# Attention heads in pairs between a layer's products, on one core

## Chip, core and metric

One core of one Trainium2 chip runs one layer of a decoder. The metric is the device time of one execution in microseconds; the median of the runs counts. TensorE is the engine of matrix products, VectorE, ScalarE and GpSimd work on tiles, SyncE issues the transfers of weights. In the profile they are PE (PEld: its weight loads), DVE, ACT, POOL and SP.

## What is computed

256 positions of width 2048, batch 1, float32. The reference, cut to what matters:

```python
h = rmsnorm(x, mix_norm_g)
qkv = h @ w_in                              # 2048 x 6144: q, k, v of group A, then of group B
q_a, k_a = partial_rope(q_a), partial_rope(k_a)     # first quarter of each head, 8 heads of 128
o_a = moba_attention(q_a, k_a, v_a)         # 256 positions are one block: causal softmax
o_b = stick_breaking_attention(q_b, k_b, v_b)       # 8 heads, no softmax, strictly causal
x = x + concat(rmsnorm(o_a, moba_out_g), rmsnorm(o_b, sb_out_g)) @ w_out
x = x + square(relu(rmsnorm(x, mlp_norm_g) @ w_up)) @ w_down
out = rmsnorm(x, final_norm_g)
```

## The kernel before

**Products.** All weights come in items of 512 rows by 512 columns, one step for each. Item i+3 is fetched into `raw` while item i is worked on. Each weight is split into a high and a low float32r part: ScalarE writes `wh` (`split_hi`, L122), VectorE writes the rest `wl` (`split_lo`, L128), each in two halves of an item, two items ahead of the products (LOOK = 2). In `w_stationary` (q, k and w_up; L234, L235) the weights are loaded into TensorE and the activations stream, 16 pairs of products a step; in `x_stationary` (v, w_out, w_down; L250 to L252) it is the other way round, 24 products a step. The products add up in six buffers `acc` of PSUM.

**Order.** The order of the work is written out by hand (`manual_schedule`); each engine runs its own instructions in the order in which they were issued, and waits only for data and buffers. `step` issues an item: half of its products, what hangs on hook 2i, the split of the first half of item i+2 on VectorE, the other half of the products, what hangs on hook 2i+1, the split of the second half. `at(slot, f, ...)` hangs f on a hook, and it is issued there on all engines that it uses. So what a hook issues on VectorE stands in VectorE's queue ahead of the split that follows.

**Heads.** The heads go in four groups of four: stick-breaking heads 0 to 3 and 4 to 7 (gi = 0, 1), then MoBA heads 0 to 3 and 4 to 7 (gi = 2, 3). Each group has 12 items, four of q, four of v, four of k. Its attention runs during the 12 items of the next group, hung on hooks counted from i0, the hook in the middle of the first of them: hooks 0 to 7 belong to q's items, 8 to 15 to v's, 16 to 23 to k's. The fourth group's attention runs among the items of w_out (eight for each half of the heads; hooks 0 to 15 are the first eight). A head's attention is in three places on TensorE:

- `probs` (L339 to L369): `scores` (L333, L334), four matmuls that take q and k; then for stick-breaking two sigmoids on ScalarE, causal masks on GpSimd, scans and a product on VectorE (L351, L354; the scanned tiles `stay` and `cum` have one buffer), and for MoBA the softmax: mask and scale (L361), maxima (L363), exponentials on ScalarE (L364), reciprocal (L366), scaling (L368);
- `turn` (L375): three transposes of the probabilities, copied out by ScalarE (L377);
- `values` (L385, L386): four matmuls with v, then the output's split and its squares for the norm on ScalarE, VectorE and GpSimd (L391 to L395).

Each place takes a buffer of `att`, of which there are two.

**q and k.** When a q or k item group ends, `qk_out` (L318, L319) puts the sums of each head into qT or kT. `qk_scale` multiplies them by the norm's factor on GpSimd (L329); for MoBA heads it first rotates the first 32 dimensions on VectorE (L325 to L328, four instructions on 32 partitions). For k's head 0 it is issued at once, for heads 1 to 3 it hangs on a hook ahead of the head's scores.

Before the change these hooks were, with `gap, d1, d2 = (3, 4, 5) if gi == 3 else (4, 5, 7)`:

```python
at(2 * state["i"] + gap * m - 1, qk_scale, dst, m, rope)     # k, heads 1 to 3
at(i0 + 2 + gap * m, probs, qT, kT, m, box)
at(i0 + 2 + gap * m + d1, turn, m, box, tbox)
at(i0 + 2 + gap * m + d2, values, g, h, m, vs, tbox)
```

In the first three groups that gives scores at hooks 2, 6, 10, 14, turnings at 7, 11, 15, 19, values at 9, 13, 17, 21 and k's scaling at 3, 7, 11; in the fourth, scores at 2, 5, 8, 11, turnings at 6, 9, 12, 15, values at 7, 10, 13, 16 and k's scaling at 2, 5, 8. A residual add of w_out (`o_out`, L448) is issued by the products themselves, ahead of the hook that follows them.

Of the kernel before, what the change touches and what calls it, by code (L numbers as in the profile page):

```python
# [49 lines left out]
def layer(ctx: ExitStack, tc, x, mix_g, w_in, moba_g, sb_g, w_out, mlp_g, w_up, w_down, fin_g,  # L50
# [84 lines left out]
    def rms_scale(r, ss, n):  # L135

        nc.vector.tensor_scalar(r, ss, 1.0 / n, EPS, op0=ALU.mult, op1=ALU.add)
        nc.gpsimd.tensor_tensor(r, r, mhalf[:, :r.shape[-1]], op=ALU.pow)
# [86 lines left out]
    def w_stationary(i, ps, j, nj, done):  # L225

        wh, wl = parts[i]
        mk = [(m, k) for m in range(4) for k in range(KI)]
        if i < 3:
            mk = [(m, k) for k in range(KI) for m in range(4)]  # L230
        for n, (m, k) in enumerate(mk):
            kt = j * KI + k
            first, last = j == 0 and k == 0, j == nj - 1 and k == KI - 1
            nc.tensor.matmul(ps[m], wh[:, k, m * P:(m + 1) * P], actT[:, kt, :], start=first, stop=False)  # L234
            nc.tensor.matmul(ps[m][:, S:2 * S], wl[:, k, m * P:(m + 1) * P], actT[:, kt, 0:S],  # L235
                             start=False, stop=last)
            if last:
                done(m)
            if n == (3 if i < 3 else 7) or (i == 0 and n == 7):
                yield  # L240
        parts.pop(i)
# [14 lines left out]
    def x_stationary(i, ps, j, nj, xT, k0, done):  # L256
        for t in range(2):
            x_part(i, ps, j, nj[t], xT, k0, t, done)
            if t == 0:
                yield  # L260
        parts.pop(i)
# [4 lines left out]
    def at(slot, f, *a):  # L266

        hooks.setdefault(slot, []).append((f, a))
# [5 lines left out]
    state = {"i": 0}  # L274

    def step(work):
        i = state["i"]
        state["i"] += 1
        fetch(i + 3)
        h0, h1 = slice(0, KI // 2), slice(KI // 2, KI)  # L280
        ahead = i + LOOK if i >= LOOK else len(items)
        if i > LOOK:
            split_hi(ahead, h0)
        for part, _ in enumerate(work(i)):
            run_hooks((i, part) if part else 2 * i)
            split_hi(ahead, h1 if i > LOOK else slice(0, KI))
            split_lo(ahead, h0)
        run_hooks(2 * i + 1)
        split_lo(ahead, h1)
        del raws[i]  # L290
# [13 lines left out]
    with ExitStack() as phase:  # L304
# [10 lines left out]
        def qk_out(dst, ps, m):  # L315

            low = aw.tile([P, S], F32, name="low")
            nc.scalar.copy(low, ps[:, S:2 * S])  # L318
            nc.vector.tensor_add(dst[:, m, :], ps[:, 0:S], low)  # L319

        def qk_scale(dst, m, rope):

            if rope:
                rot = aw.tile([32, 2, S], F32, name="rot", bufs=1)
                nc.vector.stream_shuffle(rot[:, 0], dst[:32, m, :], [(r + HALF) % 32 for r in range(32)])  # L325
                nc.vector.tensor_mul(rot[:, 0], rot[:, 0], sinr)
                nc.vector.tensor_mul(rot[:, 1], dst[:32, m, :], cosr)
                nc.vector.tensor_add(dst[:32, m, :], rot[:, 0], rot[:, 1])  # L328
            nc.gpsimd.tensor_mul(dst[:, m, :], dst[:, m, :], r1b)  # L329
# [67 lines left out]
        def group_scale(g):  # L397
# [3 lines left out]
            nc.vector.tensor_copy(rg[:, g, :], ps[:, 0:2])  # L401
            rms_scale(rg[:, g, :], rg[:, g, :], DG)

        for gi, (g, h) in enumerate(((1, 0), (1, 1), (0, 0), (0, 1))):
            rope = g == 0
            gap, d1, d2 = (3, 4, 5) if gi == 3 else (4, 5, 7)
            qT = qkvp.tile([P, 4, S], F32, name="qT")
            kT = qkvp.tile([P, 4, S], F32, name="kT")
            vs = qkvp.tile([P, 2, CW], F32, name="vs")
            def v_out(t):  # L410
                if t == 0:
                    nc.scalar.activation(vs[:, 0, :], ps[0], AF.Copy, scale=r1[:, 0:1])
                else:
                    nc.vector.tensor_scalar(vs[:, 1, :], ps[1], r1[:, 1:2], None, op0=ALU.mult)

            def head_out(kind, m):
                dst = qT if kind == "q" else kT
                qk_out(dst, ps[m], m)
                if kind == "q":
                    at(2 * state["i"] + (6 if gi == 0 else 0) + 2 * m, qk_scale, dst, m, rope)  # L420
                elif m == 0:
                    qk_scale(dst, m, rope)
                else:
                    at(2 * state["i"] + gap * m - 1, qk_scale, dst, m, rope)

            for kind in "qvk":
                ps = [acc.tile([P, 512], F32, name="acc") for _ in range(2 if kind == "v" else 4)]
                for j in range(4):
                    if kind == "v":
                        step(lambda i: x_stationary(i, ps, j, (4, 4), actT, 0, v_out))  # L430
                    else:
                        step(lambda i: w_stationary(i, ps, j, 4, lambda m: head_out(kind, m)))
            box, tbox = {}, {}
            i0 = 2 * state["i"]
            probs = probs_moba if g == 0 else probs_sb
            for m in range(4):
                at(i0 + 2 + gap * m, probs, qT, kT, m, box)
                at(i0 + 2 + gap * m + d1, turn, m, box, tbox)
                at(i0 + 2 + gap * m + d2, values, g, h, m, vs, tbox)
            if h == 1:  # L440
                at(i0 + 2 + gap * 3 + d2 + 2, group_scale, g)


        ssx = op.tile([P, 2, 4], F32, name="ssx")
# [133 lines left out]
```

## Time and profile before

| what | before |
|---|---|
| median of 3 runs | 1108.91 us (1108.74 to 1108.95) |
| the profiled execution | 1109.04 us, its span 1107.3 us |
| TensorE busy | 1096.8 us, 99% of the span |
| VectorE, ScalarE, GpSimd busy | 634.0, 506.4, 130.3 us (57%, 46%, 12%) |
| chain that ended last | TensorE 97%, transfers 1% |
| granted clock of TensorE, mean | 0.998 |
| transfers | 207.96 MB, 188 GB/s in the mean |

Matmuls follow each other before the one ahead has ended, so what a product costs is read from the start of one to the start of the next, not from its duration. In brackets at a row's end stands how long the engine was idle before it and what ended that. A row of a timeline that stands for several equal instructions ends in their number (x3), and its duration is that of all of them.

### The profile page before, as it was taken

To read this page: it belongs to the slowest core of one execution; us is meant where nothing else is said; L and a number is where in the kernel's file an instruction comes from. 1 tells how busy PE (TensorE), PEld (TensorE's weight loads), DVE (VectorE), ACT (ScalarE), POOL (GpSimd) and SP (SyncE) were. 2 spreads that over 40 slices of the span, in tenths; PEclk is the share of its full clock that TensorE was granted. 3 is DMA by queue.
4 is the path that set the end of the run, shared out by engine and by line. 5 is a ranking of instruction groups with operands and counts; after the bars stand their busy time and mean duration, and the time that the engine had idled before them with its cause. 6 is when DMAs were issued, how large, how long until landed. Compare 5 with 4: busy or idle time off the path is not lost.

```text
span 1107.3 us, 14123 instructions
## 1 busy us (share of the span) xinstructions
PE 1096.8 (99%) x5672; PEld 938.3 (85%) x5672; DVE 634.0 (57%) x818; ACT 506.4 (46%) x735; POOL 130.3 (12%) x154
## 2 busy tenths in 40 slices
PE   8999999999999999999999999999999999999997
PEld 7888888888888888888888888888888888888886
DVE  5655657668676665655564444445655565455453
ACT  5645444455444554544453333334444544344342
POOL 0101213224111002211220000001111211000000
PEclk9999999999999999999999999999999999999999
DMA  8755454554545554666457546554665456555642
GB/s 304 243 163 181 155 188 156 188 190 153 184 158 190 187 192 154 213 225 206 154 174 245 190 155 226 190 190 152 207 214 188 152 207 212 190 200 188 207 165 76
DMA packets 104673, 207.96 MB, mean 188 GB/s; under 512 B 3440, under 2 KB 4512, under 8 KB 104480
## 3 DMA queue, kind: packets, MB, share of 16 engines
q1 hardware_dynamic: 103376, 204.49, 54.5%
q10 hardware_dynamic: 1232, 2.58, 0.7%
q8 instruction: 44, 0.72, 0.3%
q14 instruction: 21, 0.17, 0.0%
HBM read 204.96 MB, written 2.10 MB: 187 GB/s over the span
## 4 chain that ended last, share of the span: by engine, by line
PE 97%; DMA 1%; issue 0%; ACT 0%; SPq 0%; DVE 0%; POOLq 0%; POOL 0%; ACTq 0%
PE acc L234 31%; PE acc L235 16%; PE acc L252 16%; PE acc L250 16%; PE acc L251 16%; DMA raw<-in_w_in 1%; PE att L334 1%; PE att L385 1%; PE att L375 0%; PE att L150 0%; PE att L386 0%; PE att L333 0%; SPq L113 0%; ACT xs L522 0%; DVE wl L128 0%
## 5 line engine op out<-in xcount | busy, mean ns | idle before, releaser
L128 DVE TENSOR_TENSOR wl<-raw,wh 128x1024 fp32r<-128x1024 f32 (+1 forms) x386 | 461.5, 1231 | 198.0 <-ACT wh L122 198.0
L122 ACT ACTIVATE wh<-raw 128x1024 fp32r<-128x1024 f32 (+1 forms) x385 | 389.5, 1051 | 351.0 <-PE acc L252 202.0
L234 PE MATMUL acc<-actT,wh 128*128 128x512 f32 x1536 | 536.8, 394 | 0.6 <-ACT wh L122 0.6
L235 PE MATMUL acc<-actT,wl 128*128 128x256 f32 x1536 | 429.9, 280 | 0.4 <-DVE wl L128 0.4
L234 PEld LDWEIGHTS acc<-actT,wh 128*128 128x128 f32 x1536 | 288.4, 188 | 63.9 <-ACT wh L122 0.9
L235 PEld LDWEIGHTS acc<-actT,wl 128*128 128x128 f32 x1536 | 288.6, 188 | 1.3 <-DVE wl L128 1.0
L250 PE MATMUL acc<-wh,uT 128*128 128x512 f32 (+1 forms) x520 | 200.7, 386 | 0.0
L251 PE MATMUL acc<-wl,uT 128*128 128x512 f32 (+1 forms) x520 | 200.7, 386 | 0.0
L252 PE MATMUL acc<-wh,uT 128*128 128x512 f32 (+1 forms) x520 | 200.7, 386 | 0.0
L488 POOL TENSOR_TENSOR uT<-u,uT 128x256 fp32r<-128x256 f32 x64 | 61.3, 958 | 510.0 <-ACT uT L487 510.0
L251 PEld LDWEIGHTS acc<-wl,uT 128*128 128x128 f32 x520 | 97.7, 188 | 19.8
L250 PEld LDWEIGHTS acc<-wh,uT 128*128 128x128 f32 x520 | 97.7, 188 | 19.7
L252 PEld LDWEIGHTS acc<-wh,uT 128*128 128x128 f32 x520 | 97.7, 188 | 19.4
L485 DVE TENSOR_TENSOR u<-acc,ulow 128x256 f32<-128x256 f32 x64 | 27.2, 425 | 99.7 <-ACT ulow L484 89.8
L487 ACT ACTIVATE uT<-u 128x256 fp32r<-128x256 f32 x64 | 26.8, 418 | 67.0 <-DVE u L486 67.0
L250 PE MATMUL acc<-wh,actT 128*128 128x512 f32 x128 | 52.6, 411 | 0.0
L250 PE MATMUL acc<-wh,oT 128*128 128x512 f32 x128 | 51.8, 405 | 0.0
L252 PE MATMUL acc<-wh,actT 128*128 128x512 f32 x128 | 50.2, 392 | 0.0
L252 PE MATMUL acc<-wh,oT 128*128 128x512 f32 x128 | 50.1, 391 | 0.0
L251 PE MATMUL acc<-wl,actT 128*128 128x512 f32 x128 | 49.9, 390 | 0.0
L251 PE MATMUL acc<-wl,oT 128*128 128x512 f32 x128 | 49.9, 390 | 0.0
L491 DVE SCALAR_TENSOR_TENSOR xs<-acc,r,xs 128x512 f32<-128x512 f32 (+1 forms) x18 | 13.0, 720 | 43.2 <-PE acc L252 43.2
(106 smaller groups left out, 574.4 us busy)
## 6 DMA issues: line engine op xcount, KB each, us to landing
raw<-in_w_up SPq DMA_DIRECT2D x64, 1024.0 KB, 6.1
raw<-in_w_down SPq DMA_DIRECT2D x64, 1024.0 KB, 5.1
raw<-in_w_in SPq DMA_DIRECT2D x47, 1024.0 KB, 5.2
raw<-in_w_out SPq DMA_DIRECT2D x16, 1024.0 KB, 5.0
xs<-in_x SPq DMA_DIRECT2D x3, 512.0 KB, 9.1
raw<-in_w_in SPq DMA_DIRECT2D x4, 256.0 KB, 5.7
fgb<-in_final_norm_g ACTq DMA_DIRECT2D x1, 1024.0 KB
out<-xs SPq DMA_DIRECT2D x4, 256.0 KB, 2.4
```

Source lines behind the costliest of these rows:

```text
L122: nc.scalar.activation(parts[i][0][:, ks], raws[i][:, ks], AF.Copy)
L128: nc.vector.tensor_sub(wl[:, ks], raws[i][:, ks], wh[:, ks].bitcast(F32))
L234: nc.tensor.matmul(ps[m], wh[:, k, m * P:(m + 1) * P], actT[:, kt, :], start=first, stop=False)
L235: nc.tensor.matmul(ps[m][:, S:2 * S], wl[:, k, m * P:(m + 1) * P], actT[:, kt, 0:S], start=False, stop=last)
L250: nc.tensor.matmul(ps[t][:, :cols.stop - cols.start], hi, wh[:, k, cols], start=first, stop=False)
L251: nc.tensor.matmul(ps[t][:, :cols.stop - cols.start], hi, wl[:, k, cols], start=False, stop=False)
L252: nc.tensor.matmul(ps[t][:, :cols.stop - cols.start], lo, wh[:, k, cols], start=False, stop=last)
L334: nc.tensor.matmul(ps[:, P:3 * P], qT[:, m, P:S], kT[:, m, :], start=True, stop=True)
L485: nc.vector.tensor_add(u, ps[:, 0:S], low)
L487: nc.scalar.activation(hi, u, AF.Copy)
L488: nc.gpsimd.tensor_sub(lo, u, hi.bitcast(F32))
L491: nc.vector.scalar_tensor_tensor(xs[:, t, c0:c1], ps[:, :c1 - c0], r2[:, t:t + 1], xs[:, t, c0:c1], op0=ALU.mult, op1=ALU.add)
```

## The change

The hooks of the four groups come from a table, by pairs of heads. Heads 0 and 1 have their scores at one hook, their turnings at one hook and their values at one hook, and so have heads 2 and 3: in the first three groups at hooks 2, 7, 16 and 5, 17, 19, in the fourth at 2, 8, 10 and 5, 11, 14. That makes 6 places of a group in place of 12. The scaling of k's heads 1, 2 and 3 hangs on hooks 1, 3 and 4. The norm of a group's output (`group_scale`) follows two hooks after the last values, as before.

```diff
+        WHEN = (((2, 7, 16), (5, 17, 19)), ((2, 8, 10), (5, 11, 14)))
         for gi, (g, h) in enumerate(((1, 0), (1, 1), (0, 0), (0, 1))):
             rope = g == 0
-            gap, d1, d2 = (3, 4, 5) if gi == 3 else (4, 5, 7)
+            when = WHEN[gi == 3]
...
                 elif m == 0:
                     qk_scale(dst, m, rope)
                 else:
-                    at(2 * state["i"] + gap * m - 1, qk_scale, dst, m, rope)
+                    at(2 * state["i"] + (0, 1, 3, 4)[m], qk_scale, dst, m, rope)
...
             probs = probs_moba if g == 0 else probs_sb
-            for m in range(4):
-                at(i0 + 2 + gap * m, probs, qT, kT, m, box)
-                at(i0 + 2 + gap * m + d1, turn, m, box, tbox)
-                at(i0 + 2 + gap * m + d2, values, g, h, m, vs, tbox)
+            for pair, (t_probs, t_turn, t_values) in enumerate(when):
+                for m in (2 * pair, 2 * pair + 1):
+                    at(i0 + t_probs, probs, qT, kT, m, box)
+                    at(i0 + t_turn, turn, m, box, tbox)
+                    at(i0 + t_values, values, g, h, m, vs, tbox)
             if h == 1:
-                at(i0 + 2 + gap * 3 + d2 + 2, group_scale, g)
+                at(i0 + t_values + 2, group_scale, g)
```

How the instructions then stand, engine by engine. VectorE in the third group (gi = 2, MoBA) before, from the end of head 0's softmax to the start of head 1's; L128 is a split, L325 to L328 the rotation of a k head, L319 puts q's sums into qT:

```order
L368 TENSOR_SCALAR prob<-prob,st 128x256
L128 TENSOR_TENSOR wl<-raw,wh 128x1024
L325 STREAM_SHUFFLE rot<-kT 32x256
L326 TENSOR_TENSOR rot<-rot,cst 32x256
L327 TENSOR_TENSOR rot<-kT,cst 32x256
L328 TENSOR_TENSOR kT<-rot 32x256
L128 TENSOR_TENSOR wl<-raw,wh 128x1024 x3
L319 TENSOR_TENSOR qT<-acc,low 128x256 x2
L361 SCALAR_TENSOR_TENSOR prob<-att,cst 128x384
```

One rotation, head 1's, lay between two softmaxes, with four splits and two sums around it. VectorE at the same place with the change, from the start of head 1's softmax to the start of head 2's:

```order
L361 SCALAR_TENSOR_TENSOR prob<-att,cst 128x384
L363 TENSOR_REDUCE st<-prob 128x1 x2
L366 RECIPROCAL st<-st 128x2
L368 TENSOR_SCALAR prob<-prob,st 128x128
L368 TENSOR_SCALAR prob<-prob,st 128x256
L128 TENSOR_TENSOR wl<-raw,wh 128x1024
L325 STREAM_SHUFFLE rot<-kT 32x256
L326 TENSOR_TENSOR rot<-rot,cst 32x256
L327 TENSOR_TENSOR rot<-kT,cst 32x256
L328 TENSOR_TENSOR kT<-rot 32x256
L128 TENSOR_TENSOR wl<-raw,wh 128x1024
```

Head 0's softmax, the same five rows, stands directly ahead of these. The rotation shown is head 2's; behind the last row come head 3's four rows, one more split, and then the softmax of head 2. Head 1's rotation has moved ahead of head 0's softmax.

VectorE in the fourth group (among w_out's items) with the change, from the split behind head 2's rotation on; L452 is the residual add, L448 before:

```order
L128 TENSOR_TENSOR wl<-raw,wh 128x1024
L452 SCALAR_TENSOR_TENSOR xs<-acc,rg,xs 128x512
L325 STREAM_SHUFFLE rot<-kT 32x256
L326 TENSOR_TENSOR rot<-rot,cst 32x256
L327 TENSOR_TENSOR rot<-kT,cst 32x256
L328 TENSOR_TENSOR kT<-rot 32x256
L128 TENSOR_TENSOR wl<-raw,wh 128x1024
L452 SCALAR_TENSOR_TENSOR xs<-acc,rg,xs 128x512
L361 SCALAR_TENSOR_TENSOR prob<-att,cst 128x384
```

The first row is the split behind head 2's rotation, the rotation shown is head 3's, and the last row begins head 2's softmax. Before, the piece of the queue with head 3's rotation was this (L393 is of a head's values):

```order
L393 SCALAR_TENSOR_TENSOR oT<-att,g_85,oT 128x256
L128 TENSOR_TENSOR wl<-raw,wh 128x1024
L325 STREAM_SHUFFLE rot<-kT 32x256
L326 TENSOR_TENSOR rot<-rot,cst 32x256
L327 TENSOR_TENSOR rot<-kT,cst 32x256
L328 TENSOR_TENSOR kT<-rot 32x256
L361 SCALAR_TENSOR_TENSOR prob<-att,cst 128x384
```

Head 3's rotation stood ahead of head 2's softmax, three hooks ahead of head 3's own scores, and no residual add lay between the split and the rotation; now it stands one hook ahead of its scores, behind the softmaxes of heads 0 and 1 and a residual add.

On TensorE, the first scores of the third group then stand as two heads' in a row between L235 and L234, and the scores of heads 2 and 3 three half steps behind them; each head's scores wait for GpSimd's multiplication of its own k alone.

## Rows read from the trace of the kernel before

**Rows 1.** The page: busy time by engine, and the chain that ended last.

```profile
PE 1096.8 (99%) x5672; PEld 938.3 (85%) x5672; DVE 634.0 (57%) x818; ACT 506.4 (46%) x735; POOL 130.3 (12%) x154
...
PE 97%; DMA 1%; issue 0%; ACT 0%; SPq 0%; DVE 0%; POOLq 0%; POOL 0%; ACTq 0%
```

**Rows 2.** Waits of TensorE: who for whom, us in total, times, longest us.

```profile
PE acc L203 <- POOL mhalf L81: 1.5, 1, 1.5
...
PE att L150 <- DVE actT L156: 0.4, 1, 0.4
```

**Rows 3.** TensorE's timeline, scores, then turning: start us, us, instruction.

```profile
98.43 0.38 PE L333 MATMUL att<-kT,qT 128*128 128x128 f32 x2
...
99.32 0.28 PE L235 MATMUL acc<-actT,wl 128*128 128x256 f32 x1
...
139.18 0.28 PE L235 MATMUL acc<-actT,wl 128*128 128x256 f32 x1
...
139.87 0.28 PE L235 MATMUL acc<-actT,wl 128*128 128x256 f32 x1
```

**Rows 4.** The same at scores, third and then fourth group, heads 0 and 1.

```profile
233.22 0.38 PE L333 MATMUL att<-kT,qT 128*128 128x128 f32 x2
...
244.97 0.38 PE L333 MATMUL att<-kT,qT 128*128 128x128 f32 x2
...
306.14 0.38 PE L333 MATMUL att<-kT,qT 128*128 128x128 f32 x2
...
314.99 0.38 PE L333 MATMUL att<-kT,qT 128*128 128x128 f32 x2
```

**Rows 5.** The page, groups: busy us, mean ns of one, idle before.

```profile
L250 PE MATMUL acc<-wh,uT 128*128 128x512 f32 (+1 forms) x520 | 200.7, 386 | 0.0
...
L250 PE MATMUL acc<-wh,actT 128*128 128x512 f32 x128 | 52.6, 411 | 0.0
```

**Rows 6.** VectorE's timeline, third group, then fourth: softmax, splits, rotation, residual add.

```profile
234.07 0.56 DVE L361 SCALAR_TENSOR_TENSOR prob<-att,cst 128x384 f32<-128x384 f32 x1 [4.44 <-PE att L334]
...
236.67 1.22 DVE L128 TENSOR_TENSOR wl<-raw,wh 128x1024 fp32r<-128x1024 f32 x1
...
237.81 0.44 DVE L325 STREAM_SHUFFLE rot<-kT 32x256 f32<-32x256 f32 x1
...
239.41 3.48 DVE L128 TENSOR_TENSOR wl<-raw,wh 128x1024 fp32r<-128x1024 f32 x3
...
307.00 0.56 DVE L361 SCALAR_TENSOR_TENSOR prob<-att,cst 128x384 f32<-128x384 f32 x1 [2.54 <-PE att L334]
...
309.60 2.35 DVE L128 TENSOR_TENSOR wl<-raw,wh 128x1024 fp32r<-128x1024 f32 x2
...
315.18 0.75 DVE L448 SCALAR_TENSOR_TENSOR xs<-acc,rg,xs 128x512 f32<-128x512 f32 x1 [0.77 <-PE acc L252]
```

**Rows 7.** Timeline of GpSimd at three multiplications of a k head.

```profile
239.56 3.94 POOL L329 TENSOR_TENSOR kT<-kT,r1b 128x256 f32<-128x256 f32 x1 [11.63 <-DVE kT L328]
...
252.06 1.66 POOL L329 TENSOR_TENSOR kT<-kT,r1b 128x256 f32<-128x256 f32 x1 [8.56 <-DVE kT L328]
...
304.54 0.74 POOL L329 TENSOR_TENSOR kT<-kT,r1b 128x256 f32<-128x256 f32 x1 [5.14 <-DVE kT L328]
```

**Rows 8.** Timeline of ScalarE, first group: head 1's second sigmoid.

```profile
99.67 0.48 ACT L343 ACTIVATE stay<-att 128x384 f32<-128x384 f32 x1
```

**Rows 9.** Timeline of VectorE, first group: head 1's scans, the split behind.

```profile
100.55 1.84 DVE L351 TENSOR_TENSOR_SCAN cum<-stay,onesw 128x128 f32<-128x128 f32 x2 [1.09 <-POOL stay L348]
...
103.26 1.21 DVE L128 TENSOR_TENSOR wl<-raw,wh 128x1024 fp32r<-128x1024 f32 x1
```

**Rows 10.** Stretches at the end: length, busy us by engine, granted clock, DMA.

```profile
1100.00:1104.00 4.00, 0.00 (x0) 0.00 (x0) 1.69 (x5) 1.74 (x4) 0.56 (x1) 0.97 0.39 143
1104.00:1107.30 3.30, 0.00 (x0) 0.00 (x0) 0.00 (x0) 0.00 (x0) 0.00 (x0) 0.50 0.59 212
```

**Rows 11.** Timeline of TensorE: the first warm-up transposes.

```profile
1.51 2.82 PE L203 MATMUL acc<-ident 128*128 128x128 f32 x12 [1.51 <-POOL mhalf L81]
```

## Prediction

> **What bounds it now.** Read the page first: TensorE is busy in 99% of the span, and the chain that ended last is 97% TensorE [rows 1]. The waits of TensorE come next: five in all, the longest 1.5 us, all before or among the first products [rows 2]. So nothing that the attention does is late today; TensorE's own stream sets the end, and there are two ways to change the time: make that stream shorter, or put a wait into it. For the first I read the timeline of TensorE around a place of the attention, for the second the timelines of VectorE, GpSimd and ScalarE around the same places.
>
> Hooks are counted as above, hook n of a group being i0 + n. One head's scores cost TensorE 0.66 us: from their start (98.43) to the second product behind them (99.32) it is 0.89 us, of which 0.23 is the first product's [rows 3]. Half a step of q or k products takes (244.97 - 233.22 - 0.66) / 4 = 2.77 us (8 such pairs of products, 0.35 us each), half a step of w_out's (314.99 - 306.14 - 0.66) / 3 = 2.73 us, 12 products of 0.23 us [rows 4].
>
> **What the change saves.** Each of the four groups has 12 places now and 6 then, 24 fewer. A turning costs 139.87 - 139.18 - 0.35 = 0.34 us [rows 3] and streams half as many columns as the scores. Twice 0.34 less 0.66 leaves 0.02 us for entering and leaving a place, so 0.5 us for 24. Besides, the products near a place may run a little slower: an L250 lasts 411 ns in the mean with actT, 18 of which stand right behind a place, and 386 ns with uT, where there are no places [rows 5]; most of these 25 ns is the first product waiting for the attention's last columns, which moves along with them. Bounds: the gain is nothing at the least; at the most, an estimate, a third of the 25 ns does not move along, for 256 products (v's and w_out's) 2 us, 2.5 us with the 0.5. I take **0.7 us**, near to the 0.02 us that the starts show.
>
> **What it adds: a late k.** The scores of heads 2 and 3 come at hook 5 now, before at hooks 10 and 14 (8 and 11 in the fourth group). They wait for kT[2] and kT[3], whose scaling is issued at hooks 3 and 4. In the two MoBA groups the scaling is a rotation (four VectorE instructions), then a multiplication on GpSimd, and in VectorE's queue it now stands behind the softmax of both heads 0 and 1, as the order of VectorE's instructions shows.
>
> *Third group* (times of the trace before; all work up to there stays). Head 0's softmax begins at 234.07 and lets the next split start at 236.67, 2.60 us later [rows 6]. Head 1's follows in the queue: to 239.27. A split holds the queue 1.14 us (236.67 to 237.81): 240.41. Rotation of head 2, 1.60 us (237.81 to 239.41): 242.01. Split: 243.15. Then the rotation of head 3, and a split behind it.
> GpSimd starts 0.15 us behind a rotation (239.41 to 239.56). It takes 0.74 us where VectorE does not split (304.54), 1.66 us where one split began just ahead of it (252.06) and 3.94 us beside three of them (239.56) [rows 7]. Here one split stands behind each rotation, so a key is ready 1.60 + 0.15 + 1.66 = 3.41 us after its rotation began: kT[2] at 240.41 + 3.41 = 243.82, kT[3] at 243.15 + 3.41 = 246.56.
> TensorE would reach hook 5 at 233.22 + 2 x 0.66 + 3 x 2.77 = 242.85. Head 2's scores wait till 243.82 and end at 244.48, head 3's wait till 246.56: 0.97 + 2.08 = **3.0 us**.
>
> *Fourth group*, the same among w_out's products: the softmax from 307.00, 2.60 us a head [rows 6]: 312.20; split: 313.34; head 2 ready at 313.34 + 3.41 = 316.75; the next split from 314.94 to 316.08. Then a residual add (L448 before, L452 now; 0.75 us [rows 6]) stands ahead of head 3's rotation: 316.83, ready at 320.24. TensorE at hook 5: 306.14 + 1.32 + 8.19 = 315.65. Waits: 1.10, scores to 317.41, then 2.83: **3.9 us**.
>
> TensorE has no idle time behind these places that could absorb a wait, so 6.9 us reach the end whole. Bounds: were GpSimd never held up (0.74 us), a key would be ready 2.49 us after its rotation began; the waits of head 2 all but vanish (0.05 and 0.18) and head 3's keep 2.08 and 2.83: 5.1 us. If every multiplication took 3.94 us, the last key of each group came 2.28 us later: 11.5 us. I take the case of one split behind, since the order has just one there.
> A rule to weigh: the Trainium skill, page "SBUF — State Buffer", section "Who interferes with whom", says that a VectorE instruction with two inputs in SBUF and a GpSimd one exclude each other, and whichever issues first runs alone. By it, with GpSimd first, the split would wait some 0.8 us and the sum be 5.1 + 2 x 0.8 = 6.7 us; row 252.06 shows GpSimd as the one that waits.
>
> **What it does not add.** A pair takes both buffers of att; values at hook 16 and turnings at 17 are half a step apart, 2.77 us, in which the two heads' values can be read out. Head 1's key is rotated at hook 1, ahead of the softmax, where VectorE was idle 4.44 us (until 234.07 [rows 6]): in time. Fetches and splits stay in their order.
>
> **Rivals.** (a) *Keys in time.* If VectorE had head 3's rotation done 3 us (third group) and 3.9 us (fourth) earlier, nothing would wait: 1108.9 - 0.7 = 1108.2 us, not slower. For it: those 4.44 us of idle VectorE, and head 1's softmax could run where head 0's waits for ScalarE. Against it: the softmax needs the scores, which come at hook 2, and the queue is in order. 12%.
> (b) *The stick-breaking groups wait too.* There a key needs no rotation, but a head's scans wait for GpSimd and for the one buffer `stay`. A head takes 4.83 us from its scores (98.43) to the next split (103.26). The second head's sigmoid waits for the first one's scans, to 102.39; from that sigmoid to the scans it is 0.88 us (99.67 to 100.55), then 2.71 us to the split: 105.98, 7.55 us after the scores [rows 3, 8, 9]. The split that follows at hook 5 is the second half of the first weights for v: done 8.7 us after hook 5. TensorE wants it after 1.32 (scores) + 5.54 (a step) + 0.68 (two turnings) + 1.6 (7 products): 9.1 us. That fits by 0.4 us, which a slow GpSimd would eat in both groups: 1.5 us in all, 1116.7 us. 13%.
> (c) *The clock falls in the waits.* After TensorE's last product, before 1100, the granted clock still is 0.97 in the mean of 1100 to 1104; at half, 1.2 GHz, it is after that [rows 10]. The waits here are shorter than those four us. At half clock a transpose takes some 0.22 us (twelve in 2.82 us at the start [rows 11]) and 0.11 in a turning, and the start was spent so for 3 us: 1.5 us lost by a fall, 3 us by two, 1118.2 us. 6%. The Trainium skill, page "TensorE: Matmul & The Clock Gate", section "What's actually happening", says that an idle TensorE is put to half clock until it has been busy again; the row of 1104 agrees, and no row shows a fall within the work.
> (d) *The change does not do what it says.* The first turnings stand just ahead of v's first product and the first values half a step behind v's last; so it holds in three groups, and in the fourth all places lie among w_out's. This moves no number above.
>
> **The numbers.** The sum is made against the profiled execution, 1109.04 us (span 1107.3): 1109.04 - 0.7 + 3.0 + 3.9 = 1115.2; the median of the runs is 0.13 lower, so **1115.1 us**. Chances: the forecast 69%, (a) 12%, (b) 13%, (c) 6%. A measurement of this kernel can tell about 0.2%, 2.2 us, from no change; (a) lies within that, unless the gain is at its upper bound: faster 2%, same 10%, slower 88%. The range: from 1112.0 (GpSimd not held up gives 1113.3, a larger gain up to 1.3 less) to 1118.0 (GpSimd held up longer, or (b) and a fall of the clock); it leaves out (a) and about half of (c).
>
> **What would show it.** Right: TensorE waits for GpSimd's kT (L329) ahead of scores, four times, some 1.0, 2.1, 1.1 and 2.8 us, at about 243 to 247 and, shifted by the first three microseconds, 319 to 324; VectorE goes from one head's softmax straight into the next. Wrong: no wait of TensorE on kT, which is (a); a wait on the splits at v's first products, which is (b); a granted clock under 1.00 between 240 and 330, which is (c); or waits shorter by 1.8 us in sum, if GpSimd is not held up.

## The result, and the profile after

| what | before | after |
|---|---|---|
| median of 6 runs | 1108.96 us (1108.74 to 1109.4) | 1118.53 us (1117.16 to 1120.34) |
| the profiled execution | 1109.04 us, span 1107.3 us | 1118.12 us, span 1116.2 us |
| mean granted clock | 0.998 | 0.995 |

After to before is 1.0086, with a 95% interval of 1.0075 to 1.0097: 9.6 us slower. The forecast of 1115.1 had the sign and the place; its range ended at 1118.0, 0.5 us short. The six executions lie far apart, from 1117.16 us at a mean clock of 0.997 to 1120.34 us at 0.992.

The page of the changed kernel, busy time and chain, answers to [rows 1]:

```profile
PE 1100.5 (99%) x5672; PEld 941.6 (84%) x5672; DVE 633.0 (57%) x818; ACT 506.6 (45%) x735; POOL 133.9 (12%) x154
...
PE 96%; DVE 2%; ACT 1%; issue 1%; POOL 0%; POOLq 0%; ACTq 0%
```

The chain now runs through TensorE for 96% of the span, before for 97%. TensorE's waits in the changed kernel (who for whom, us in total, times, longest) answer to [rows 2] and say where:

```profile
PE att L333 <- POOL kT L329: 6.1, 4, 2.5
```

This line is new: four waits of scores for a key from GpSimd. The timeline of TensorE in the changed kernel (start, duration, instruction, in brackets the idle time ahead), second pair's scores in the third group, then in the fourth, beside [rows 4]:

```profile
241.79 0.28 PE L235 MATMUL acc<-actT,wl 128*128 128x256 f32 x1
242.90 0.49 PE L333 MATMUL att<-kT,qT 128*128 128x128 f32 x2 [0.82 <-POOL kT L329]
...
245.68 0.80 PE L333 MATMUL att<-kT,qT 128*128 128x128 f32 x2 [1.86 <-POOL kT L329]
...
246.76 0.99 PE L234 MATMUL acc<-actT,wh 128*128 128x512 f32 x1
...
248.81 0.28 PE L235 MATMUL acc<-actT,wl 128*128 128x256 f32 x1
...
318.90 0.39 PE L252 MATMUL acc<-wh,oT 128*128 128x512 f32 x1
320.23 0.49 PE L333 MATMUL att<-kT,qT 128*128 128x128 f32 x2 [0.94 <-POOL kT L329]
...
323.62 0.61 PE L333 MATMUL att<-kT,qT 128*128 128x128 f32 x2 [2.47 <-POOL kT L329]
...
324.53 0.99 PE L250 MATMUL acc<-wh,oT 128*128 128x512 f32 x1
...
327.37 0.40 PE L250 MATMUL acc<-wh,oT 128*128 128x512 f32 x1
```

By starts, as the forecast counts: head 2's scores are due 0.12 us after 241.79 (a product of 256 columns) and begin 0.99 us late; head 3's are due at 242.90 + 0.66 and begin 2.12 late. In the fourth group it is 1.10 and 2.73. Forecast were 1.0, 2.1, 1.1 and 2.8. The brackets are shorter because they count from the modelled ends.

But the waits are not all. The product behind the scores lasts 0.99 us, where 0.39 is usual; the fourth scores stream in 0.91 us (323.62 to 324.53), where one head's matmuls at full speed take 0.66 [rows 3]. Here is the granted clock of the changed kernel by stretches (from:to, length, busy us of TensorE, weight loads, VectorE, ScalarE, GpSimd; then the clock, 1.00 for 2.4 GHz and 0.50 for 1.2 GHz, and two figures on transfers):

```profile
243.60:245.30 1.70, 0.22 (x2) 0.00 (x0) 1.70 (x3) 0.00 (x0) 1.32 (x1) 1.00 0.82 265
245.40:248.70 3.30, 3.02 (x9) 2.65 (x10) 2.41 (x9) 1.12 (x5) 0.22 (x1) 0.50 0.40 156
...
320.90:323.80 2.90, 0.43 (x3) 0.18 (x2) 2.87 (x6) 0.00 (x0) 1.65 (x1) 1.00 0.96 343
323.90:327.20 3.30, 3.30 (x10) 2.64 (x10) 2.41 (x9) 1.01 (x5) 0.00 (x0) 0.50 0.01 4
```

In head 3's wait TensorE stands; at 245.3, and in the fourth group just behind the wait at 323.8, the clock goes to its lower level, 1.2 GHz, and stays there for 3.3 us in which TensorE is busy nearly throughout. That is rival (c), on top of the forecast and not in place of it.

VectorE, the timeline of the changed kernel, beside [rows 6]. Third group: head 0's softmax, the split, head 2's rotation, the split, head 3's rotation, its end; fourth group: the residual add and head 3's rotation behind it.

```profile
233.12 0.56 DVE L361 SCALAR_TENSOR_TENSOR prob<-att,cst 128x384 f32<-128x384 f32 x1 [3.16 <-PE att L334]
...
238.31 1.22 DVE L128 TENSOR_TENSOR wl<-raw,wh 128x1024 fp32r<-128x1024 f32 x1
...
239.46 0.43 DVE L325 STREAM_SHUFFLE rot<-kT 32x256 f32<-32x256 f32 x1
...
241.05 1.21 DVE L128 TENSOR_TENSOR wl<-raw,wh 128x1024 fp32r<-128x1024 f32 x1
...
242.19 0.42 DVE L325 STREAM_SHUFFLE rot<-kT 32x256 f32<-32x256 f32 x1
...
243.83 1.21 DVE L128 TENSOR_TENSOR wl<-raw,wh 128x1024 fp32r<-128x1024 f32 x1
...
319.52 0.73 DVE L452 SCALAR_TENSOR_TENSOR xs<-acc,rg,xs 128x512 f32<-128x512 f32 x1
...
320.19 0.42 DVE L325 STREAM_SHUFFLE rot<-kT 32x256 f32<-32x256 f32 x1
```

And GpSimd, the two keys of the third group, beside [rows 7]:

```profile
241.20 1.64 POOL L329 TENSOR_TENSOR kT<-kT,r1b 128x256 f32<-128x256 f32 x1 [10.63 <-DVE kT L328]
243.98 1.65 POOL L329 TENSOR_TENSOR kT<-kT,r1b 128x256 f32<-128x256 f32 x1 [1.13 <-DVE kT L328]
```

Two softmaxes take 5.19 us (5.20 forecast), a split 1.15 and 1.14, a rotation 1.59 and 1.64, a key's scaling 0.15 + 1.65. In the fourth group the residual add holds head 3's rotation up for 0.67 us (0.75 forecast). The queue is the forecast's, step by step. Beside one split it was GpSimd that waited; the splits kept their length.

### The profile page after: what moved, and what is told of

Its sections match the earlier page's. It is cut to its first block, busy times and chain, and to the rows that moved or that the text cites. A ratio compares the mean times of both kernels' runs of the same rounds, so it can differ in the third digit from the quotient of the medians.

```text
span 1116.2 us, 14136 instructions
## 1 busy us (share of the span) xinstructions
PE 1100.5 (99%) x5672; PEld 941.6 (84%) x5672; DVE 633.0 (57%) x818; ACT 506.6 (45%) x735; POOL 133.9 (12%) x154
## 4 chain that ended last, share of the span: by engine, by line
PE 96%; DVE 2%; ACT 1%; issue 1%; POOL 0%; POOLq 0%; ACTq 0%
PE acc L234 31%; PE acc L235 16%; PE acc L250 15%; PE acc L252 15%; PE acc L251 15%; PE att L150 1%; PE att L385 1%; PE att L334 1%; DVE wl L128 0%; PE att L375 0%; ACT prob L364 0%; PE att L333 0%; PE att L386 0%; POOL kT L329 0%; PE acc L203 0%
## 5 line engine op out<-in xcount | busy, mean ns | idle before, releaser
L128 DVE TENSOR_TENSOR wl<-raw,wh 128x1024 fp32r<-128x1024 f32 (+1 forms) x386 | 462.0, 1232 | 204.3 <-ACT wh L122 204.2
L234 PE MATMUL acc<-actT,wh 128*128 128x512 f32 x1536 | 537.5, 394 | 0.0
L235 PE MATMUL acc<-actT,wl 128*128 128x256 f32 x1536 | 429.9, 280 | 0.1
L234 PEld LDWEIGHTS acc<-actT,wh 128*128 128x128 f32 x1536 | 288.9, 188 | 63.2
L235 PEld LDWEIGHTS acc<-actT,wl 128*128 128x128 f32 x1536 | 288.8, 188 | 1.3 <-DVE wl L128 0.7
L250 PE MATMUL acc<-wh,actT 128*128 128x512 f32 x128 | 50.3, 393 | 0.0
L252 PE MATMUL acc<-wh,actT 128*128 128x512 f32 x128 | 49.9, 390 | 0.0
```

What stands on the lines that cost most here:

```text
L128: nc.vector.tensor_sub(wl[:, ks], raws[i][:, ks], wh[:, ks].bitcast(F32))
L250: nc.tensor.matmul(ps[t][:, :cols.stop - cols.start], hi, wh[:, k, cols], start=first, stop=False)
L252: nc.tensor.matmul(ps[t][:, :cols.stop - cols.start], lo, wh[:, k, cols], start=False, stop=last)
```

## Experiments

In all of them a median belongs to 5 to 11 runs of the kernel, and the kernel before had medians of 1109.11, 1109.01 and 1108.97 us in the three sessions. The hooks of k's scaling are the tuple `(0, 1, 3, 4)[m]` in L427.

**e1: keys early.** In the MoBA groups all keys are rotated before the softmaxes.

```diff
-at(2 * state["i"] + (0, 1, 3, 4)[m], qk_scale, dst, m, rope)
+at(2 * state["i"] + ((0, 1, 1, 1) if rope else (0, 1, 3, 4))[m], qk_scale, dst, m, rope)
```

> In the two MoBA groups the keys of heads 2 and 3 are rotated and scaled at hook 1, ahead of the softmax of heads 0 and 1; everything else is as in the changed kernel. Theory (the late keys are the whole loss, partly as waits and partly as the clock that falls in them): no wait of TensorE on kT, granted clock 1.00 from 240 to 345 us, and the time of the kernel before less what the 24 places save. In the changed kernel's trace the two places at hook 5 and the products right behind them cost 10.2 us more than their streaming, and the span grew by 8.9, so 1.3 us are saved: 1107.7 us (by the prediction's 0.7 it would be 1108.2). Rival (pairs cost something by themselves, in slower products around them or in splits that come late): 1109.5 us or more, with the waits gone.

Measured: 1108.64 us, ratio 0.9996 (0.9987 to 1.0004). No wait on kT, so the loss hangs on the late keys, and pairs by themselves cost nothing that this measurement can tell. The 1107.7 was too low, in part because it set one profiled span against another, and the changed kernel's profiled execution, 1118.12, lies 0.4 us under its median. The same two places, from the last product ahead of the scores to the sixth behind them (seventh in the fourth group), in the timeline of TensorE of e1:

```profile
242.29 0.28 PE L235 MATMUL acc<-actT,wl 128*128 128x256 f32 x1
...
244.65 0.28 PE L235 MATMUL acc<-actT,wl 128*128 128x256 f32 x1
...
314.74 0.39 PE L252 MATMUL acc<-wh,oT 128*128 128x512 f32 x1
...
317.66 0.40 PE L250 MATMUL acc<-wh,oT 128*128 128x512 f32 x1
```

2.36 and 2.92 us; in the changed kernel 7.02 (241.79 to 248.81) and 8.47 (318.90 to 327.37). So the places cost 4.66 + 5.55 = 10.2 us more, of which the medians show 9.6: by this reckoning the change saves 0.6 us elsewhere.

**e2 and e5: TensorE busy in the waits.** How much of the 10.2 is the clock? TensorE transposes the identity into unused columns while it waits; `fill` is 8 for head 2, and for head 3 it is 17 (third group) or 24 (fourth).

```diff
 def scores(qT, kT, m, fill=0):
     ps = att.tile([P, 512], F32, name="att")
+    for _ in range(fill):
+        nc.tensor.transpose(ps[:, 3 * P:], ident, ident)
```

> The changed kernel, but TensorE turns the identity into the unused last 128 columns of the scores' own buffer while it waits in the MoBA groups: 8 turnings (0.11 us each) ahead of head 2's scores, 17 ahead of head 3's in the third group and 24 in the fourth, all a little shorter than the waits. Theory (two parts: the waits of 1.0, 2.1, 1.1 and 2.7 us, and on top of them a clock that falls because TensorE stands still): scores start when they did, the clock stays full, and the time is 1107.7 + 6.9 = 1114.6 us (1114.0 to 1115.3). Rival (what came on top of the waits is not from standing still: the clock falls for another reason, or the scores and the products behind them are slow for want of operands): 1118.5 us as before. Rival (the fillers themselves delay): above 1118.5.

Measured: 1116.55 us, 2 us better than the changed kernel and 2 us worse than hoped. Of that, 0.9 us is the base of 1107.7, which e1 had at 1108.64. Another part was a slip: `fill` was read when the place was issued, by then with the fourth group's value, so 24 turnings ran in the third group too and ended some 0.6 us after the key was there. e5 mends it.

> The busy wait of e2 once more, with 17 turnings ahead of head 3's scores in the third group as was meant there (e2 ran 24 in both groups, and in the third they ended 0.65 us after the key was ready). Theory (waits of 3.0 and 3.9 us as forecast, and a clock that falls because TensorE stands still in them): no start of scores later than the key, granted clock 1.00 throughout, 1108.64 (keys early) + 7.0 = 1115.6 us; what is left to the changed kernel's 1118.5 is the clock. Rival (the fillers change nothing but the clock record, and e2's time came from elsewhere): above 1116.3 us. Rival (the waits are longer than forecast and the clock is the smaller part): no shorter than e2.

Measured: 1115.6 us (1115.26 to 1116.18), as the theory had it. TensorE's timeline in e5, both groups:

```profile
242.23 0.28 PE L235 MATMUL acc<-actT,wl 128*128 128x256 f32 x1
...
243.34 0.49 PE L335 MATMUL att<-kT,qT 128*128 128x128 f32 x2
...
244.10 2.02 PE L334 MATMUL att<-ident 128*128 128x128 f32 x17
246.13 0.49 PE L335 MATMUL att<-kT,qT 128*128 128x128 f32 x2
...
247.82 0.28 PE L235 MATMUL acc<-actT,wl 128*128 128x256 f32 x1
...
317.90 0.40 PE L252 MATMUL acc<-wh,oT 128*128 128x512 f32 x1
...
324.77 0.39 PE L250 MATMUL acc<-wh,oT 128*128 128x512 f32 x1
```

Its granted clock there:

```profile
241.00:248.00 7.00, 6.99 (x50) 6.11 (x49) 6.04 (x15) 0.99 (x4) 3.31 (x2) 1.00 0.48 152
318.00:328.00 10.00, 9.93 (x63) 8.56 (x62) 8.21 (x22) 2.81 (x9) 2.84 (x2) 1.00 0.34 107
```

The keys come as late as before, the clock stays full, and the same two stretches take 5.59 and 6.87 us. That parts the loss of this profiled execution: waits (5.59 - 2.36) + (6.87 - 2.92) = **7.2 us**, clock (7.02 - 5.59) + (8.47 - 6.87) = **3.0 us**. The medians agree: e5 less e1 is 7.0 us, the changed kernel less e5 is 2.9 us.

**e3: scaling on VectorE.** The keys of heads 2 and 3 are multiplied on VectorE, behind their rotation.

```diff
-nc.gpsimd.tensor_mul(dst[:, m, :], dst[:, m, :], r1b)
+eng = nc.vector if vec else nc.gpsimd
+eng.tensor_mul(dst[:, m, :], dst[:, m, :], r1b)
...
-at(2 * state["i"] + (0, 1, 3, 4)[m], qk_scale, dst, m, rope)
+at(2 * state["i"] + (0, 1, 3, 4)[m], qk_scale, dst, m, rope, rope and m > 1)
```

> The changed kernel, but the keys of heads 2 and 3 in the MoBA groups are scaled on VectorE, right behind their rotation, and not on GpSimd. Theory (the queue of VectorE, with two softmaxes and two rotations ahead, sets the waits; GpSimd's hold-up is the smaller part): head 2's waits vanish, head 3's key comes some 0.9 us earlier in each group (0.45 us for the multiplication, an estimate between the 0.436 of a 32x256 product and the 0.650 of a 128x383 one, in place of 0.15 + 1.65): waits of 2.2 and 2.9 us stay. With a full clock 1107.7 + 5.1 = 1112.8; with a fall in each of the two waits, as in the changed kernel (1.7 us each), 1116.1. Rival (GpSimd sets them): no wait left, 1107.7.

Measured: 1115.74 us. In e3 TensorE waits twice, for head 3's keys, as its list of waits has it:

```profile
PE att L334 <- DVE kT L330: 5.1, 2, 2.9
```

VectorE multiplies in 0.42 us, by its timeline:

```profile
241.44 0.42 DVE L330 TENSOR_TENSOR kT<-kT,r1b 128x256 f32<-128x256 f32 x1
```

So VectorE's queue, not GpSimd, sets most of the wait: 5.1 us of the 6.1 stay. By starts e3's two waits are 2.3 and 3.1 us; 1108.64 + 5.4 + 1.5 for one fall is 1115.5. The clock of e3 beside those two waits, third group and fourth:

```profile
243.10:245.50 2.40, 0.31 (x3) 0.34 (x4) 2.30 (x6) 0.00 (x0) 0.00 (x0) 1.00 0.48 97
245.60:248.90 3.30, 3.30 (x12) 2.72 (x11) 2.44 (x8) 0.98 (x4) 0.00 (x0) 0.50 0.60 234
319.60:322.40 2.80, 0.00 (x0) 0.00 (x0) 2.70 (x9) 0.00 (x0) 0.00 (x0) 1.00 0.51 156
322.50:326.00 3.50, 3.50 (x17) 2.94 (x18) 2.71 (x5) 0.99 (x4) 0.00 (x0) 1.00 0.43 164
```

It fell behind the shorter wait and not behind the longer one. Length alone doesn't decide it.

**e4: pairs in the stick-breaking groups alone** (the MoBA groups take the hooks of before).

```diff
 for m in (2 * pair, 2 * pair + 1):
+    if rope:
+        t_probs = 2 + gap * m
+        t_turn, t_values = t_probs + d1, t_probs + d2
```

> Pairs in the two stick-breaking groups alone; the two MoBA groups as in the kernel before. Theory (pairing is harmless where no key is rotated, and saves half of what it saves in all): 1108.96 - 0.65 = 1108.3 us, no wait on kT. By the prediction's 0.7 for all four groups it would be 1108.6. Rival (the stick-breaking groups carry a part of the loss: a second head that waits for the one buffer stay, and splits for v behind it): above 1109.5.

Measured: 1108.64 us, ratio 0.9996 (0.9987 to 1.0005), no wait on kT, and for a split one of 0.6 us, at 15 us among the first products. Rival (b) falls.

**e6: only head 2's key late**, `(0, 1, 3, 1)[m]` in the MoBA groups.

> In the two MoBA groups head 3's key is rotated at hook 1, head 2's stays at hook 3, behind the softmax. Two short waits are left, of 1.0 us in the third group and 1.1 us in the fourth, where the changed kernel has four. Theory A (waits add up one for one, and the clock falls only in the long ones): 1108.64 + 2.1 = 1110.7 us, clock 1.00 from 240 to 345. Theory B (any wait of this size may drop the clock, as long ones do): 1110.7 + 1.0 to 1.7 a fall, 1112.4 to 1114.1 us.

Measured: 1111.91 us (1111.74 to 1113.52), 1.2 us above theory A, but with a full clock in both groups of the profile. The wait was mis-sized: e6's timeline of TensorE in the third group:

```profile
244.65 0.49 PE L333 MATMUL att<-kT,qT 128*128 128x128 f32 x2 [1.96 <-POOL kT L329]
```

And that of GpSimd there:

```profile
241.81 2.78 POOL L329 TENSOR_TENSOR kT<-kT,r1b 128x256 f32<-128x256 f32 x1 [8.76 <-DVE kT L328]
```

With head 3's rotation gone, two splits stand in a row behind head 2's, and the same multiplication takes 2.78 us, not 1.64. By starts head 2 waits 2.1 us in the third group and 1.1 in the fourth; 1108.64 + 3.2 = 1111.8. So the waits add up one for one here, and a wait of 2.1 us can leave the clock full. One execution of seven took 1113.52; a fall would explain it, but no trace of it was taken.

**e7 and e9: keys late, scores later.** In e7 the second pair's scores of the MoBA groups come at hook 7.

```diff
 for pair, (t_probs, t_turn, t_values) in enumerate(when):
+    if rope and pair:
+        t_probs = 7
```

> The keys stay where the changed kernel has them (hooks 3 and 4, behind the softmax of the first pair); in the MoBA groups the scores of the second pair move from hook 5 to hook 7, the other places stay. Theory (a late key costs only because the scores come too early for it): hook 7 is two half steps, 5.5 us, later, the last key is 3.1 us late in the third group and 3.8 us in the fourth, so no wait on kT, a full clock, and the time of the kernel with the keys early, 1108.6 us. Rival (the order on VectorE and GpSimd costs something besides, for instance splits that come late behind two softmaxes and two rotations): above 1109.6.

Measured: 1110.17 us. No wait on kT, but new ones in e7's list of TensorE's waits:

```profile
PE att L375 <- DVE prob L361: 1.3, 1, 1.3
...
PE att L333 <- ACT aT L377: 0.3, 1, 0.3
```

The scores now stand beside turnings, and the two buffers of att are taken: a cost of the place that was chosen, 1.6 us. e9 keeps them apart: scores at hook 8 in the third group, at 7 in the fourth with the first pair's turnings at 6.

> As e7 (keys where the changed kernel has them, the second pair's scores of the MoBA groups later), but with the buffers of att free for them: in the third group the scores come at hook 8, a half step behind the turnings of hook 7, and in the fourth at hook 7, with the first pair's turnings moved from hook 8 to hook 6. In e7 scores and turnings stood side by side there, and TensorE waited for the buffers: 1.3 us ahead of a turning, 0.3 us ahead of scores. Theory (a late key costs only where its scores come before it): no wait on kT nor at those turnings, a full clock, 1108.6 us as with the keys early. Rival (the order on VectorE costs something besides): above 1109.6.

Measured: 1108.28 us (1108.14 to 1108.48), ratio 0.9994 (0.9984 to 1.0003), with no wait but the start's and 0.7 us for splits. Within what a measurement can tell, a late key costs only what its scores come too early for it. e1 and e9 both lie 0.5 to 0.7 us below the kernel before, less than a measurement can tell for sure.

**e8: keys early in the third group alone**, `((0, 1, 1, 1) if gi == 2 else (0, 1, 3, 4))[m]`.

> Keys early (hook 1) in the third group alone; the fourth group as in the changed kernel, with its waits of 1.1 and 2.8 us. Theory (the two groups' losses are independent and add up): waits of 3.9 us and one fall of the clock of up to 1.7 us: 1108.64 + 3.9 = 1112.5 without a fall, 1113.6 to 1114.2 with it. Rival (the fall in the fourth group follows from the one in the third): 1112.5 us, clock 1.00.

Measured: 1114.01 us, the theory's 1113.6 to 1114.2. The clock of e8 in the third group and in the fourth:

```profile
240.00:250.00 10.00, 10.00 (x60) 8.85 (x59) 7.82 (x16) 5.55 (x15) 0.00 (x0) 1.00 0.34 107
...
318.00:321.30 3.30, 1.32 (x7) 1.19 (x8) 3.08 (x6) 0.42 (x3) 1.65 (x1) 1.00 0.72 278
321.40:324.70 3.30, 3.30 (x9) 2.53 (x8) 1.94 (x7) 1.64 (x7) 0.00 (x0) 0.50 0.00 0
```

It falls in the fourth without a fall in the third, and the time is that of one group's loss: the two losses are independent. And it falls late, as TensorE's timeline in e8 shows:

```profile
319.98 0.49 PE L333 MATMUL att<-kT,qT 128*128 128x128 f32 x2 [2.47 <-POOL kT L329]
```

With head 3's scores TensorE had been at work again for 1.4 us when the clock fell.

**e10: the changed kernel again.**

> The changed kernel itself once more, for a second profile and more executions. Theory (the waits are the same in every execution, 7.0 us; how often the clock falls in them is not, and makes the spread): waits on kT of the same lengths to 0.1 us, a time of 1115.6 us plus 1.3 to 1.7 for each fall, so about 1118.6 with two, 1117.2 with one, and lower mean clocks in the slower executions. Rival (the clock falls at fixed places, like the waits): two falls at the same two places, and executions that agree within 0.3 us as those of the kernel with the keys early do.

Measured: 1116.81, 1116.99, 1117.23 us with mean clocks of 0.997, and 1118.67, 1118.99 with 0.995. The profiled one is 1118.67. Its list of waits has the same line on kT as the changed kernel's above. Its clock behind them:

```profile
246.00:249.20 3.20, 2.96 (x9) 2.58 (x10) 2.31 (x9) 1.05 (x5) 0.19 (x1) 0.50 0.42 163
324.40:327.80 3.40, 3.40 (x10) 2.74 (x10) 2.51 (x9) 1.07 (x5) 0.00 (x0) 0.50 0.05 17
```

The waits repeat to the tenth; the times make two clusters, 1.8 us apart, which go with the clock. The profile shows two falls at 1118.67. That the executions at 1117.0 had one is read from 1115.6 + 1.5, not from a trace; a mean clock of 0.997 alone doesn't show it, for e9's profile has that too, with a full clock from 10 to 1099 us. A third fall would explain the 1120.34 us of the first session in the same way; no trace shows it.

## Why the prediction was wrong

- **The saving, -0.7 us.** Not contradicted: -0.6 by the medians and the two places, -0.5 and -0.7 in e1 and e9. None of them is clear of no change, and e4, with half of the places saved, has the same 1108.64 us as e1. (By the forecast's own bound of 2.5 us the gain could be 1.8 us larger, not 1.3 as in the range's lower end; nothing hung on it.)
- **Third and fourth group, +3.0 and +3.9 us.** Right: 3.2 and 3.95 in e5. The order on VectorE, the 1.65 us of GpSimd beside one split and the residual add in the fourth group all came as reckoned. GpSimd's hold-up lay where [rows 7] put it; e6 shows that it moves with the number of splits behind the rotation.
- **"What it does not add."** Right: the stick-breaking groups wait for nothing (e4), the fetches keep pace.
- **(a), (b), (d).** None happened. (a) is what e1 makes of the kernel by putting the rotations ahead of the softmaxes.
- **(c), the clock: the step that failed.** The sum put it at nothing; the runs show 3.0 us, two falls of 1.4 and 1.6 us in the traced execution. Its price was right, 1.5 us a fall and 3 for two, 1118.2 us against 1118.53, though it rested on the slow transposes of the start, for which the profile's clock column reads 1.00 (1.50:4.30 of the kernel before). It was given 6%, because "the waits here are shorter than those four us" of [rows 10]. Four us were one sample of the program's end. The clock behind the last product in e6, where that product began at 1102.15:

```profile
1102.60:1104.40 1.80, 0.00 (x0) 0.00 (x0) 0.52 (x2) 0.51 (x2) 0.56 (x1) 1.00 0.41 146
1104.60:1109.00 4.40, 0.00 (x0) 0.00 (x0) 1.10 (x3) 1.05 (x2) 0.00 (x0) 0.50 0.66 238
```

The same in e8, where it began at 1104.63:

```profile
1105.00:1109.80 4.80, 0.00 (x0) 0.00 (x0) 1.87 (x5) 1.74 (x4) 0.56 (x1) 1.00 0.49 179
1109.90:1112.00 2.10, 0.00 (x0) 0.00 (x0) 0.00 (x0) 0.00 (x0) 0.00 (x0) 0.50 0.58 211
```

From the start of the last product the clock stayed full for some 2.3 us there and 5.2 us here. A figure that varies so much from trace to trace can't exclude a fall in waits of 2.1 and 2.8 us; the sum should have held one or two falls as likely, 1116.6 to 1118.2 us, and the range should have gone past two. Its upper end allowed for one, together with (b). Without the clock the forecast would have stood: e5 has 1115.6 us, 1115.1 were predicted. By how much the range was missed is partly chance: the same kernel's median of five executions in e10, 1117.23 us, lies inside it, since three of its five executions took some 1117.0 us. But all eleven executions of the kernel took longer than the 1115.1 us of the sum that held no fall.

The Trainium skill, page "TensorE: Matmul & The Clock Gate", section "What's actually happening", says that the throttled state is the default and that activity releases it. The stretch from 323.9 agrees: TensorE was at work in all of 3.30 us, at half clock, and by 327.37 the products ran at their usual pace again. So a fall costs time in the work behind the wait, on top of the wait itself. The same section says that the point of a transition varies from run to run. It says so of the rise at a kernel's start, and no run here shows it for the falls of one kernel: in both traces of the changed kernel the clock fell 0.2 us behind the start of head 3's scores of the fourth group. In another kernel, e8, it fell 1.4 us behind it.

What stays open is what decides whether the clock falls in a given wait. By the brackets it fell in 1.86 us (third group, changed kernel) and not in 1.96 (e6), fell in 2.47 us (fourth group) and not in 2.9 (e3). Nor is it the sum of a group's waits, for e3 has one in each group and the clock fell behind the one of 2.16 us. Of the eight waits of two microseconds or more (by starts) in the kept traces without busy work in them, six were followed by a fall. It was not tried whether the kernel's earlier work, or the moment at which a wait begins, has a part in it.

## What to carry to other kernels

When a producer's step and its reader are moved nearer to each other, walk the producer's queue through in order, with each instruction's measured time, and compare with the reader's hour: here that gave four waits to within a tenth of a microsecond. A wait of TensorE of two microseconds has two prices, its length and perhaps a fall of the clock behind it (1.4 to 1.6 us each here); a forecast should hold both, and treat a delay that one execution shows as one sample. The remedy cost nothing here: issue the short step ahead of the long one in the same queue (e1), or move the reader to a place where it has buffers (e9).

## What was not expected of the hardware

- The clock fell inside a kernel whose TensorE is 99% busy, at waits of 2.1 to 2.8 us, and not each time; 25 to 32 turnings of the identity into a spare corner of a buffer kept it full and gave 2.9 us back (e5).
- One multiplication of 128x256 on GpSimd takes 0.74 us without splits [rows 7], 1.65 beside one and 2.78 beside two (e6), so that taking work out of VectorE's queue made a key later.
